# Attention row maxima in one chained pass: bias or mask added on VectorE, with the other part's extreme as the initial value

## The chip, the cores and the metric

One core of a Trainium2 chip runs the whole kernel. The metric is device time in microseconds (us) of one execution. The engines are named as the profile names them: PE (TensorE: matmuls, with PEld for its weight loads), DVE (VectorE), ACT (ScalarE), POOL (GpSimd) and SP (SyncE, which issues most of the transfers).

## The reference, cut to what matters

The model is a two-layer backbone over 512 latent tokens (an 8 x 64 grid) and 256 context tokens, of width 1024 with 16 heads of 64. Each layer is half a SwiGLU, a token mixer and another half SwiGLU. Mixer 0 (layer 0) is a neighbourhood attention with a learned bias; mixer 1 (layer 1) is a windowed attention with grouped keys, a band mask and a sink logit for each head. In both, a latent query also sees all 256 context keys, and one softmax goes over all of it.

```python
# mixer 0, for the query rows r (window of 8 x 32 keys, bias or -1e30 outside)
s_win = einsum('bcqhd,bicjhd->bhcqij', q_r, k_r) + bias
s_ctx = einsum('bcqhd,bkhd->bhcqk', q_r, kc)
p = softmax(concatenate([s_win, s_ctx], -1))
o = p_win @ v_r + p_ctx @ vc
# mixer 1, for each block b of 128 queries (keys of blocks b-1, b, b+1)
s_win = where(abs(pos_q - pos_k) <= 128, einsum('bqhgd,bkhd->bhgqk', qb, kb), -1e30)
s_ctx = einsum('bqhgd,bkhd->bhgqk', qb, kc)
p = softmax(concatenate([s_win, s_ctx, sink], -1))     # the sink takes weight, it has no value
o = p_win @ vb + p_ctx @ vc
```

## The kernel before

Activations are kept with the model's width on the partitions; every fp32 product is made of three matmuls (high by high, high by low, low by high). `ffn` runs the half SwiGLUs "0a", "0b", "1a" and "1b", `na_mixer` mixer 0 and `wa_mixer` mixer 1, in the order 0a, mixer 0, 0b, 1a, mixer 1, 1b. The code issues work in program order, and a scheduler in the framework then sets the order of the instructions on each engine by its own estimate of their times. So attention is mixed on each engine with the projections (`pq`, `pk`, `vn`, `wq`) and with the output projections (`pon`, `pow`) of neighbouring steps. Once set, the order of each engine is fixed: an engine that waits holds up all that stands behind.

The scores are computed negated (the queries are scaled by -0.125), so a row maximum is a minimum here: `m` is min over the row, and ACT computes exp(m - s) with `scale=-1.0`.

Mixer 0, `lat` (L988): for each quarter of the heads (`qd`), pair (`pr`), block of 16 columns (`cb`) and head `h`, one bank of PSUM `s` takes 256 window scores and 256 context scores. DVE then takes the minimum of the context half (L1014), adds the bias to the window half and takes the minimum with it in one pass (L1015, an accumulating pass which the profile shows as two instructions, the pass and a read of the accumulator), and takes the smaller of the two 128x1 values (L1017). ACT does the exponential (L1019), DVE the reciprocal of the sum (L1020), POOL scales (L912), PE transposes (`tp`, L893), DVE or ACT copies the transposed block back (L845, L843), and PE multiplies by the values (`o`, L903).

Mixer 1, `attn` (L1155): for each of eight pairs of heads (`s`), each block `b` of 128 queries and each of its two heads there are `nw` window scores (256 in blocks 0 and 3, 384 in blocks 1 and 2) and 256 context scores. Where they fit one bank, both are in `sw` (blocks 0 and 3); otherwise the context scores are in a bank of their own, `sc` (`split`). The band mask is added on PE: a bf16 identity `idb` times the bf16 mask `mkb` is accumulated onto the first and the last 128 columns of the window (L1178, L1180). DVE takes the minimum of the row (L1188), for split blocks that of the context part too (L1184), and combines it with the sink (L1190 or L1192). ACT does the exponentials (L1200, L1202, L1204), DVE adds up the sums and takes the reciprocal (L1210 or L1213, L1214), POOL scales, PE transposes (`tpw`, `tpc`) and multiplies (`wo`). PSUM has two banks for `s` and two for `c`.

`vtile` hands out 128x256 tiles of the pool "v", nine of them, which hold the values and, in `mod_out`, a temporary.

Of the kernel before, what the change touches and what calls it, by code (L numbers as in the profile page):

```python
# [8 lines left out]
F32 = mybir.dt.float32  # L9
F32R = mybir.dt.float32r  # L10
BF16 = mybir.dt.bfloat16
# [7 lines left out]
P = 128  # L19
# [19 lines left out]
def hybrid_kernel(ctx: ExitStack, tc: tile.TileContext, h0, cc, crow, wmod, wmodt, bmod, lnp, wst,  # L39
# [13 lines left out]
    def t2(nm, tag="t2"):  # L53
        return tp.tile([P, 512], F32, tag=tag, name=nm, bufs={"t2": 6, "ln": 2, "sl": 2}[tag])
# [244 lines left out]
    def mod_out(nm, d, c0, c1, st, prm, rm=False, dd=None):  # L299
# [6 lines left out]
        if nm == "in":  # L306
            uf = t2(f"uf{nm}_{d}", "ln" if d < 3 else "t2")
        elif nm == "l0_1":
            uf = gp.tile([P, 256], F32, tag="gs", name=f"uf{nm}_{d}", bufs=6)
        elif n <= 256:  # L310
            uf = ph["S"].tile([P, 256], F32, tag="v", name=f"uf{nm}_{d}", bufs=9)
        else:
            uf = t2(f"uf{nm}_{d}")
# [29 lines left out]

    last_rstd, last_add, hold, keep_back = [None], [None], [None], [None]
# [540 lines left out]
    def vtile(nm):  # L885
        return ph["S"].tile([P, 256], F32, tag="v", name=nm, bufs=9)
# [55 lines left out]
    def na_mixer(gt):  # L942
# [45 lines left out]
        def lat(qd, pr, st, oh, ol, cbs=range(4)):  # L988
# [15 lines left out]
            for cb in cbs:  # L1004
                pts = []
                qc = slice(cb * P, (cb + 1) * P)
                for h in range(2):
# [8 lines left out]
                                                   scale=1.0, scalar=BIG, op0=ALU.add, op1=ALU.min, accum_out=m[:, 1:2])  # L1016
                    nc.vector.tensor_tensor(out=m[:, 0:1], in0=m[:, 0:1], in1=m[:, 1:2], op=ALU.min)  # L1017
                    p = t2(f"p{nm}")
                    last_exp[0] = nc.scalar.activation(p[:], ps[:], AF.Exp, bias=m[:, 0:1], scale=-1.0, accum_out=l[:, 0:1])  # L1019
# [78 lines left out]

    mkb = cp.tile([P, 2, P], BF16, name="mkb")
    idb = cp.tile([P, P], BF16, name="idb")  # L1100
    nc.vector.tensor_copy(idb[:], idn[:])

    def wa_mixer(gt):
# [6 lines left out]
        mk = t2("mk")  # L1110
        nc.sync.dma_start(mk[:, 0:256], wmask[:])
        nc.vector.tensor_copy(mkb[:].rearrange("p a b -> p (a b)"), mk[:, 0:256])
# [42 lines left out]
        def attn(s, q, oh, ol, bs=range(4), tags=("t", "mm")):  # L1155
# [8 lines left out]
            for b in bs:  # L1164
# [6 lines left out]
                mc, lc = (small("mc", f"mc{nm}"), small("lc", f"lc{nm}")) if split else (None, None)  # L1171
                pw, pc = [], []
                for h in range(2):
                    pb = bank("s", f"sw{nm}_{h}")
                    nc.tensor.matmul(pb[:, 0:nw], q[h][:, qc], k[h][:, k0:k1], start=True, stop=False)
                    nc.tensor.matmul(pb[:, 0:nw], q[h][:, qc], k[2 + h][:, k0:k1], start=False, stop=False)
                    if b > 0:
                        nc.tensor.matmul(pb[:, 0:P], idb[:], mkb[:, 0, :], start=False, stop=b == 3)  # L1178
                    if b < 3:
                        nc.tensor.matmul(pb[:, nw - P:nw], idb[:], mkb[:, 1, :], start=False, stop=True)  # L1180
                    pb2 = bank("c", f"sc{nm}_{h}")[:, 0:NC] if split else pb[:, nw:nw + NC]
                    scores(pb2, q[h], k[h], k[2 + h], qc, slice(NL, NT))
                    if split:
                        nc.vector.tensor_reduce(out=mc[:, h:h + 1], in_=pb2, axis=AX.X, op=ALU.min)  # L1184
                        pc.append(pb2)
                        pb = pb[:, 0:nw]
                    mh = m[:, h:h + 1]
                    nc.vector.tensor_reduce(out=mh, in_=pb, axis=AX.X, op=ALU.min)  # L1188
                    if split:
                        x = nc.vector.scalar_tensor_tensor(out=mh, in0=mh, scalar=mc[:, h:h + 1], in1=sink(h), op0=ALU.min, op1=ALU.min)  # L1190
                    else:
                        x = nc.vector.tensor_tensor(out=mh, in0=mh, in1=sink(h), op=ALU.min)  # L1192
                    pw.append(pb)
# [321 lines left out]
```

## Time and profile before

| | us |
|---|---|
| median of 3 runs | 2760.47 (2759.29 to 2761.58) |
| the profiled execution, its own time | 2773.53 |
| its span in the profile | 2771.7 |
| stretch of mixer 0 (taken as 615 to 1010 us) | 395 |
| stretch of mixer 1 (taken as 2080 to 2360 us) | 280 |
| PE busy over the span | 2659.9 |
| DVE / POOL / ACT busy over the span | 1857.4 / 1674.3 / 1204.9 |

The views used are: the page (busy time of each engine over the span), the busy time by stretch, the groups of instructions by line (count, busy time, mean duration, and the idle time before them with what ended it), the list of who waited for whom, and the timeline, in which each row has start, duration, engine, line, operation, and in brackets the idle time of the engine before it and what ended it. Starts follow each other more closely than durations suggest, since instructions of an engine overlap in its pipeline.

### The profile page before, as it was taken

To read this page: it belongs to the slowest core of one execution; us is meant where nothing else is said; L and a number is where in the kernel's file an instruction comes from. 1 tells how busy PE (TensorE), PEld (TensorE's weight loads), DVE (VectorE), ACT (ScalarE), POOL (GpSimd) and SP (SyncE) were. 2 spreads that over 40 slices of the span, in tenths; PEclk is the share of its full clock that TensorE was granted. 3 is DMA by queue.
4 is the path that set the end of the run, shared out by engine and by line. 5 is a ranking of instruction groups with operands and counts; after the bars stand their busy time and mean duration, and the time that the engine had idled before them with its cause. 6 is when DMAs were issued, how large, how long until landed. Compare 5 with 4: busy or idle time off the path is not lost. (4 is left out here: it accounts for less than half of the span.)

```text
span 2771.7 us, 47917 instructions
## 1 busy us (share of the span) xinstructions
PE 2659.9 (96%) x16954; PEld 2423.5 (87%) x16954; DVE 1857.4 (67%) x4250; ACT 1204.9 (43%) x2493; POOL 1674.3 (60%) x1522
## 2 busy tenths in 40 slices
PE   8999999999999989999999999999998999899997
PEld 5899998888888889999998899999986777898997
DVE  4877777775555677656565776666587667677765
ACT  5334343366446344343433434343336655444442
POOL 4786765464434556867664577767545445667762
PEclk9999999999999999999999999999998999999998
DMA  9367555422222213444453236465722111235551
GB/s 320 105 174 205 143 155 152 144 80 61 58 58 57 63 46 92 117 127 126 125 132 106 73 87 165 112 166 165 205 87 63 32 31 47 63 103 126 133 143 57
DMA packets 295615, 311.92 MB, mean 113 GB/s; under 512 B 27856, under 2 KB 193872, under 8 KB 294352
## 3 DMA queue, kind: packets, MB, share of 16 engines
q1 hardware_dynamic: 278960, 279.36, 33.8%
q0 software_dynamic: 16128, 29.37, 6.3%
q8 instruction: 134, 2.20, 0.3%
q14 instruction: 105, 0.86, 0.1%
q10 hardware_dynamic: 288, 0.14, 0.0%
HBM read 300.92 MB, written 12.25 MB: 113 GB/s over the span
## 5 line engine op out<-in xcount | busy, mean ns | idle before, releaser
L104 POOL TENSOR_TENSOR wl<-wr,wh 128x512 fp32r<-128x512 f32 x200 | 262.7, 1332 | 161.2 <-ACT wh L102 102.7
L104 POOL TENSOR_TENSOR wl_s<-S,wh_s 128x512 fp32r<-128x512 f32 x240 | 316.6, 1354 | 53.5 <-ACT wh_s L102 53.0
L102 ACT CAST wh_s<-S 128x512 fp32r<-128x512 f32 x256 | 155.9, 620 | 430.3 <-POOL S L636 151.2
L636 POOL TENSOR_TENSOR S<-wr,wr 128x512 f32<-128x512 f32 x128 | 173.6, 1356 | 191.8 <-DMA wr<-in_wst_dram 177.5
L211 DVE CUSTOM_DVE_ANT_0 jk<-wt,cb 128x512 f32<-128x512 f32 x360 | 244.5, 679 | 23.7 <-DMA wt<-in_wmodt_dram 18.9
L104 POOL TENSOR_TENSOR wl_a<-wr,wh_a 128x512 fp32r<-128x512 f32 x144 | 189.5, 1364 | 17.9 <-ACT wh_a L102 14.0
L102 ACT CAST wh_a<-wr 128x512 fp32r<-128x512 f32 x192 | 118.9, 622 | 152.8 <-PE pd1b L165 21.8
L102 ACT CAST wh<-wr 128x512 fp32r<-128x512 f32 x200 | 120.3, 617 | 85.5 <-DMA wr<-in_wst_dram 21.9
L495 DVE SCALAR_TENSOR_TENSOR z<-pd0b,gt,z 128x256 f32<-128x256 f32 (+1 forms) x168 | 97.0, 594 | 43.9 <-PE pd0b L166 43.2
L495 DVE SCALAR_TENSOR_TENSOR z<-pd1a,gt,z 128x512 f32<-128x512 f32 (+1 forms) x160 | 95.5, 613 | 39.1 <-PE pd1a L166 38.5
L912 POOL TENSOR_SCALAR p<-p,l 128x512 f32<-128x512 f32 x64 | 44.5, 697 | 110.0 <-DVE l L1020 107.5
L495 DVE SCALAR_TENSOR_TENSOR z<-pd0a,gt,z 128x512 f32<-128x512 f32 (+1 forms) x160 | 93.4, 611 | 16.5 <-PE pd0a L166 16.3
L335 POOL TENSOR_SCALAR z<-z,ag_None,ab_None 128x256 f32<-128x256 f32 (+1 forms) x78 | 62.7, 807 | 63.7 <-DVE uh L321 48.8
L636 POOL TENSOR_TENSOR S<-wr,S 128x512 f32<-128x512 f32 x64 | 90.4, 1413 | 3.5
L636 POOL TENSOR_TENSOR S<-S,wr 128x512 f32<-128x512 f32 x64 | 90.3, 1411 | 2.9
L912 POOL TENSOR_SCALAR pw<-pw,l 128x512 f32<-128x512 f32 (+1 forms) x64 | 41.2, 643 | 66.7 <-DVE l L1214 25.7
L1019 ACT ACTIVATE p<-s,m 128x512 f32<-128x512 f32 x64 | 44.0, 689 | 81.2 <-DVE m L1017 76.5
L317 ACT ACTIVATE ufl<-z,bi_None,sc_None 128x256 f32<-128x256 f32 (+1 forms) x86 | 55.3, 654 | 52.9 <-DVE z L480 51.8
L322 DVE TENSOR_TENSOR ul<-ufl,uh 128x256 fp32r<-128x256 f32 (+1 forms) x88 | 61.0, 699 | 5.1 <-ACT uh L319 3.6
L495 DVE SCALAR_TENSOR_TENSOR z<-pd1b,gt,z 128x512 f32<-128x512 f32 (+1 forms) x91 | 53.2, 618 | 11.2 <-PE pd1b L166 10.4
L211 DVE CUSTOM_DVE_ANT_0 jk<-zspare,cb 128x512 f32<-128x512 f32 x88 | 59.7, 678 | 0.5
L163 PE MATMUL vn<-wh,uh 128*128 128x256 f32 x192 | 54.9, 286 | 1.0 <-DVE nq L856 0.5
(1483 smaller groups left out, 10650.8 us busy)
## 6 DMA issues: line engine op xcount, KB each, us to landing
wr<-in_wst_dram SPq DMA_DIRECT2D x456, 256.0 KB
wt<-in_wmodt_dram SPq DMA_DIRECT2D x206, 256.0 KB
zspare<-in_wmodt_dram SPq DMA_DIRECT2D x50, 256.0 KB
wr_0b<-in_wst_dram SPq DMA_DIRECT2D x47, 256.0 KB
wr_1b<-in_wst_dram SPq DMA_DIRECT2D x47, 256.0 KB
wr_2b<-in_wst_dram SPq DMA_DIRECT2D x47, 256.0 KB
wr_3b<-in_wst_dram SPq DMA_DIRECT2D x47, 256.0 KB
wm<-in_wmod_dram SPq DMA_DIRECT2D x8, 1024.0 KB
```

The costliest lines, as they stand in the source:

```text
L102: nc.scalar.copy(hi[:], src[:])
L104: x = eng.tensor_tensor(out=lo[:], in0=src[:], in1=hi[:].bitcast(F32), op=ALU.subtract)
L163: behind(nc.tensor.matmul(ps, a[0], b[0], start=first, stop=False), in_front[0])
L211: x = nc.vector.tensor_tensor_reduce(out=junk[:], in0=w[:], in1=cb[st], scale=1.0, scalar=0.0, op0=ALU.mult, op1=ALU.add, accum_out=out[st])
L317: nc.scalar.activation(uf[:, :n], zs, AF.Identity, scale=s1, bias=s2)
L322: return hi, nc.vector.tensor_tensor(out=lo, in0=uv, in1=uo.bitcast(F32), op=ALU.subtract)
L335: nc.gpsimd.tensor_scalar(out=zs, in0=zs, scalar1=prm[2][:, d:d + 1], scalar2=prm[3][:, d:d + 1], op0=ALU.mult, op1=ALU.add)
L495: last[0] = nc.vector.scalar_tensor_tensor(out=zt(d, c0, c1), in0=pd, scalar=gt[:, d, st:st + 1], in1=zt(d, c0, c1), op0=ALU.mult, op1=ALU ...
L636: nc.gpsimd.tensor_tensor(out=t[:], in0=a[:], in1=b[:], op=o)
L912: nc.gpsimd.tensor_scalar(out=p, in0=p, scalar1=r, scalar2=0.0, op0=ALU.mult, op1=ALU.add)
L1019: last_exp[0] = nc.scalar.activation(p[:], ps[:], AF.Exp, bias=m[:, 0:1], scale=-1.0, accum_out=l[:, 0:1])
```

## The change

In mixer 0 the accumulating pass (L1015) takes the context minimum `m[:, 0:1]` as its initial value in place of a large constant, so its result `m[:, 1:2]` is the minimum of both halves, and L1017 is gone. In mixer 1 the mask is no longer added on PE. DVE makes two accumulating passes: one over the window scores, which adds the mask `mk3` (fp32: left edge, a block of zeros, right edge) with the sink as its initial value, and one over the context scores, which adds zeros (`nil`) with the first pass's result as its initial value. The plain minima (L1184, L1188) and the small combining steps (L1190, L1192) are gone. Tiles `mkb` and `idb` go, `mk3` takes 1.5 KB in each partition of the mixer's pool, and "v" has eight tiles there. The mask is loaded by two transfers, without a cast, and POOL clears the middle block once.

```diff
@@ lat (mixer 0)
                     nc.vector.tensor_reduce(out=m[:, 0:1], in_=ps[:, 256:512], axis=AX.X, op=ALU.min)
                     nc.vector.tensor_tensor_reduce(out=ps[:, 0:256], in0=ps[:, 0:256], in1=nbs[h][:, (0, 1, 1, 2)[cb], :],
-                                                   scale=1.0, scalar=BIG, op0=ALU.add, op1=ALU.min, accum_out=m[:, 1:2])
-                    nc.vector.tensor_tensor(out=m[:, 0:1], in0=m[:, 0:1], in1=m[:, 1:2], op=ALU.min)
+                                                   scale=1.0, scalar=m[:, 0:1], op0=ALU.add, op1=ALU.min, accum_out=m[:, 1:2])
                     p = t2(f"p{nm}")
-                    last_exp[0] = nc.scalar.activation(p[:], ps[:], AF.Exp, bias=m[:, 0:1], scale=-1.0, accum_out=l[:, 0:1])
+                    last_exp[0] = nc.scalar.activation(p[:], ps[:], AF.Exp, bias=m[:, 1:2], scale=-1.0, accum_out=l[:, 0:1])
@@ wa_mixer
-        mk = t2("mk")
-        nc.sync.dma_start(mk[:, 0:256], wmask[:])
-        nc.vector.tensor_copy(mkb[:].rearrange("p a b -> p (a b)"), mk[:, 0:256])
+        vbufs[0] = 8
+        mk3 = ph["S"].tile([P, 3, P], F32, tag="mk", name="mk", bufs=1)
+        nc.gpsimd.memset(mk3[:, 1, :], 0.0)
+        for i in range(2):
+            nc.sync.dma_start(mk3[:, 2 * i, :], wmask[:, i, :])
+        mk = mk3[:].rearrange("p a b -> p (a b)")
+        nil = mk3[:, 1:2, :].broadcast_to([P, 2, P])
@@ attn (mixer 1)
-                    nc.tensor.matmul(pb[:, 0:nw], q[h][:, qc], k[h][:, k0:k1], start=True, stop=False)
-                    nc.tensor.matmul(pb[:, 0:nw], q[h][:, qc], k[2 + h][:, k0:k1], start=False, stop=False)
-                    if b > 0:
-                        nc.tensor.matmul(pb[:, 0:P], idb[:], mkb[:, 0, :], start=False, stop=b == 3)
-                    if b < 3:
-                        nc.tensor.matmul(pb[:, nw - P:nw], idb[:], mkb[:, 1, :], start=False, stop=True)
+                    scores(pb[:, 0:nw], q[h], k[h], k[2 + h], qc, slice(k0, k1))
                     pb2 = bank("c", f"sc{nm}_{h}")[:, 0:NC] if split else pb[:, nw:nw + NC]
                     scores(pb2, q[h], k[h], k[2 + h], qc, slice(NL, NT))
+                    mh, mk0 = m[:, h:h + 1], 0 if b else P
+                    nc.vector.tensor_tensor_reduce(out=pb[:, 0:nw], in0=pb[:, 0:nw], in1=mk[:, mk0:mk0 + nw], scale=1.0,
+                                                   scalar=sink(h), op0=ALU.add, op1=ALU.min, accum_out=mc[:, h:h + 1])
+                    pb3 = pb2.rearrange("p (a b) -> p a b", a=2)
+                    x = nc.vector.tensor_tensor_reduce(out=pb3, in0=pb3, in1=nil, scale=1.0, scalar=mc[:, h:h + 1],
+                                                       op0=ALU.add, op1=ALU.min, accum_out=mh)
                     if split:
-                        nc.vector.tensor_reduce(out=mc[:, h:h + 1], in_=pb2, axis=AX.X, op=ALU.min)
                         pc.append(pb2)
                         pb = pb[:, 0:nw]
-                    mh = m[:, h:h + 1]
-                    nc.vector.tensor_reduce(out=mh, in_=pb, axis=AX.X, op=ALU.min)
-                    if split:
-                        x = nc.vector.scalar_tensor_tensor(out=mh, in0=mh, scalar=mc[:, h:h + 1], in1=sink(h), op0=ALU.min, op1=ALU.min)
-                    else:
-                        x = nc.vector.tensor_tensor(out=mh, in0=mh, in1=sink(h), op=ALU.min)
```

The scheduler sets the order of the engines anew. The order shows the same instructions elsewhere; it differs in the two mixers and at the seams to the steps around them. Three places follow; line numbers are those of each kernel's own file, and the numbers at the end of a name are buffer numbers.

The first is DVE in mixer 0, first quarter of the heads, first pair, third block of columns (`m0_0_2`), for both heads. Before:

```order
L1014 TENSOR_REDUCE m0_0_2_0_6908<-s0_0_2_0_6903 128x1
L1014 TENSOR_REDUCE m0_0_2_1_6928<-s0_0_2_1_6923 128x1
L1015 ISA s0_0_2_0_6903,m0_0_2_0_6908<-s0_0_2_0_6903,nb0_0_6796 128x256
L1015 ISA m0_0_2_0_6908 128x1
L1015 ISA s0_0_2_1_6923,m0_0_2_1_6928<-s0_0_2_1_6923,nb1_0_6801 128x256
L1015 ISA m0_0_2_1_6928 128x1
L1017 TENSOR_TENSOR m0_0_2_0_6908<-m0_0_2_0_6908 128x1
L1017 TENSOR_TENSOR m0_0_2_1_6928<-m0_0_2_1_6928 128x1
```

And in the changed kernel:

```order
L1014 TENSOR_REDUCE m0_0_2_0_6901<-s0_0_2_0_6896 128x1
L1014 TENSOR_REDUCE m0_0_2_1_6920<-s0_0_2_1_6915 128x1
L1015 ISA s0_0_2_0_6896,m0_0_2_0_6901<-s0_0_2_0_6896,nb0_0_6793,m0_0_2_0_6901 128x256
L1015 ISA m0_0_2_0_6901 128x1
L1015 ISA s0_0_2_1_6915,m0_0_2_1_6920<-s0_0_2_1_6915,nb1_0_6798,m0_0_2_1_6920 128x256
L1015 ISA m0_0_2_1_6920 128x1
```

The first head's value is ready two instructions into the passes, where before it waited behind the second head's pass.

The second is DVE in mixer 1, the fourth pair of heads (`s` = 3), block 1, which is split (`l3_1` are its sums; `pw` and `wol` belong to other steps). Before, from the copy ahead of it to the reciprocal of its first sum:

```order
L845 COPY pw2_3_1_24362<-tpw2_3_1_24377 128x512
L1188 TENSOR_REDUCE m3_1_24445<-sw3_1_0_24450 128x1
L1188 TENSOR_REDUCE m3_1_24445<-sw3_1_1_24461 128x1
L1190 SCALAR_TENSOR_TENSOR m3_1_24445<-m3_1_24445,mc3_1_24448,nsink_82 128x1 x2
L845 COPY pw3_0_1_24416<-tpw3_0_1_24431 128x512
L1210 SCALAR_TENSOR_TENSOR l3_1_24446<-l3_1_24446,lc3_1_24449,le3_1_24447 128x1
L1188 TENSOR_REDUCE m3_2_24515<-sw3_2_0_24520 128x1
L1184 TENSOR_REDUCE mc3_2_24518<-sc3_2_0_24525 128x1
L1214 RECIPROCAL l3_1_24446<-l3_1_24446 128x1
```

And in the changed kernel:

```order
L845 COPY pw2_3_1_24254<-tpw2_3_1_24269 128x512
L1178 ISA sw3_1_0_24341,mc3_1_24339<-sw3_1_0_24341,mk_22790,nsink_82 128x384
L1178 ISA mc3_1_24339 128x1
L1178 ISA sw3_1_1_24349,mc3_1_24339<-sw3_1_1_24349,mk_22790,nsink_82 128x384
L1178 ISA mc3_1_24339 128x1
L1181 ISA sc3_1_0_24344,m3_1_24336<-sc3_1_0_24344,mk_22790,mc3_1_24339 128x256
L1181 ISA m3_1_24336 128x1
L1181 ISA sc3_1_1_24352,m3_1_24336<-sc3_1_1_24352,mk_22790,mc3_1_24339 128x256
L1181 ISA m3_1_24336 128x1
L845 COPY pw3_0_1_24307<-tpw3_0_1_24322 128x512
L909 TENSOR_TENSOR wol1_0_24051<-wo2_0_24054,woh1_0_24050 128x512
```

Before, the context minima `mc3_1` of this block stood much earlier in the order; now the passes over `sc3_1` stand behind those over `sw3_1`.

The third is PE at the same place: the window scores of both heads. Before:

```order
L893 MATMUL tpw2_3_1_24377<-idn_74,pw2_3_1_24362 128x128 x4
L1175 MATMUL sw3_1_0_24450<-wk0_0_23049,wq1_1_0_24042 128x384
L1176 MATMUL sw3_1_0_24450<-wkl0_0_23051,wq1_1_0_24042 128x384
L1178 LDWEIGHTS idb_120
L1178 MATMUL sw3_1_0_24450<-mkb_119,idb_120 128x128
L1180 LDWEIGHTS idb_120
L1180 MATMUL sw3_1_0_24450<-mkb_119,idb_120 128x128
L1175 MATMUL sw3_1_1_24461<-wk1_0_23050,wq1_1_1_24043 128x384
L1176 MATMUL sw3_1_1_24461<-wkl1_0_23052,wq1_1_1_24043 128x384
L1178 LDWEIGHTS idb_120
L1178 MATMUL sw3_1_1_24461<-mkb_119,idb_120 128x128
```

And in the changed kernel:

```order
L893 MATMUL tpw2_3_1_24269<-idn_74,pw2_3_1_24254 128x128 x4
L869 MATMUL sw3_1_0_24341<-wk0_0_22983,wq1_1_0_23948 128x384
L870 MATMUL sw3_1_0_24341<-wkl0_0_22985,wq1_1_0_23948 128x384
L869 MATMUL sw3_1_1_24349<-wk1_0_22984,wq1_1_1_23949 128x384
L870 MATMUL sw3_1_1_24349<-wkl1_0_22986,wq1_1_1_23949 128x384
L893 MATMUL tpw3_0_0_24313<-idn_74,pw3_0_0_24304 128x128 x4
```

The mask matmuls and their weight loads are gone, 96 of each over the mixer, and the scores follow each other directly.

More of the change, by code (lines that the diff above doesn't have):

```diff
@@ L10 @@
 F32R = mybir.dt.float32r
-BF16 = mybir.dt.bfloat16
 I32 = mybir.dt.int32
@@ L310, in mod_out @@
         elif n <= 256:
-            uf = ph["S"].tile([P, 256], F32, tag="v", name=f"uf{nm}_{d}", bufs=9)
+            uf = ph["S"].tile([P, 256], F32, tag="v", name=f"uf{nm}_{d}", bufs=vbufs[0])
         else:
@@ L342, in behind @@
                 mybir.DependencyClass.NoSync, mybir.DependencyReason.DATA), reason="order")
+    vbufs = [9]
     last_rstd, last_add, hold, keep_back = [None], [None], [None], [None]
@@ L885, in vtile @@
     def vtile(nm):
-        return ph["S"].tile([P, 256], F32, tag="v", name=nm, bufs=9)
+        return ph["S"].tile([P, 256], F32, tag="v", name=nm, bufs=vbufs[0])
     def transpose(nm, p, order, tags):
@@ L1096, in na_mixer @@
         wo3(1)
-    mkb = cp.tile([P, 2, P], BF16, name="mkb")
-    idb = cp.tile([P, P], BF16, name="idb")
-    nc.vector.tensor_copy(idb[:], idn[:])
     def wa_mixer(gt):
@@ L1170, in attn @@
                 split = nw + NC > 512
-                mc, lc = (small("mc", f"mc{nm}"), small("lc", f"lc{nm}")) if split else (None, None)
+                mc, lc = small("mc", f"mc{nm}"), small("lc", f"lc{nm}") if split else None
                 pw, pc = [], []
```

## The prediction

> **What bounds the kernel now.** I read the page first, then the busy time by stretch (stretch, length, then PE, PEld, DVE, ACT and POOL busy with instructions, granted PE clock, DMA share, GB/s), and then what PE waits for in the two mixers (total us, times, longest).
>
> ```profile
> PE 2659.9 (96%) x16954; PEld 2423.5 (87%) x16954; DVE 1857.4 (67%) x4250; ACT 1204.9 (43%) x2493; POOL 1674.3 (60%) x1522
> 615.00:1010.00 395.00, 374.81 (x2866) 333.88 (x2865) 234.28 (x636) 193.92 (x452) 190.73 (x211) 0.98 0.23 63
> 2080.00:2360.00 280.00, 257.84 (x1836) 207.26 (x1837) 197.67 (x502) 162.36 (x435) 138.93 (x165) 0.97 0.16 43
> ```
>
> PE is the bound: 96% of the span, and in the mixers all but 395 - 374.8 = 20 us and 280 - 257.8 = 22 us. So only two things can move the time: less work on PE, and shorter or longer waits of PE. DVE is busy 59% of the first stretch and 71% of the second; what it gains or loses counts only where PE ends up waiting for it. Mixer 0's waits of PE that end in the attention's own chain are these:
>
> ```profile
> PE o L903 <- DVE p L845: 3.8, 4, 2.4
> PE tp L893 <- POOL p L912: 3.2, 4, 2.0
> PE s L869 <- ACT p L1019: 2.3, 3, 1.2
> PE s_c L869 <- ACT p L1019: 0.9, 1, 0.9
> ```
>
> That is 10.2 us in 12 waits. And from 2110 us on, in mixer 1:
>
> ```profile
> PE tpw L893 <- POOL pw L912: 3.4, 6, 0.7
> PE sw L1175 <- ACT pw L1200: 3.1, 4, 1.5
> PE wo L903 <- DVE pc L845: 1.4, 1, 1.4
> PE wo L903 <- DVE pw L845: 1.2, 3, 0.9
> ```
>
> Here 9.1 us in 14 waits. All stand behind the row minimum, since exponential, scaling and transposes need it.
>
> **Mixer 1, PE's part.** The 96 mask matmuls go, with their weight loads. In busy time a mask looks like 0.22 us, but instructions overlap, so I take the starts. First the end of a split block's scores with two masks, then a block with one:
>
> ```profile
> 2158.20 0.23 PE L1178 MATMUL sw<-mkb,idb 128*128 128x128 bf16 x1
> 2158.26 0.22 PE L1180 MATMUL sw<-mkb,idb 128*128 128x128 bf16 x1
> 2158.29 0.36 PE L869 MATMUL sc<-wk,wq 128*128 128x256 f32 x1
> 2158.49 0.28 PE L870 MATMUL sc<-wkl,wq 128*128 128x256 f32 x1
> ...
> 2150.39 0.28 PE L1176 MATMUL sw<-wkl,wq 128*128 128x256 f32 x1
> 2150.51 0.23 PE L1180 MATMUL sw<-mkb,idb 128*128 128x128 bf16 x1
> 2150.55 0.36 PE L869 MATMUL sw<-wk,wq 128*128 128x256 f32 x1
> 2150.76 0.28 PE L870 MATMUL sw<-wkl,wq 128*128 128x256 f32 x1
> 2150.88 0.82 PE L893 MATMUL tpw<-idn,pw 128*128 128x128 f32 x6
> ```
>
> A score matmul of 256 columns that follows another takes 0.12 us from start to start (2150.76 to 2150.88, and 2150.39 to 2150.51). With two masks ahead it is 0.29 us from the first mask to L870 (2158.20 to 2158.49): 0.09 for the masks, and 0.20 for the product behind them, which they delay. Without them 0.12 remains, so a pair of masks costs 0.17 us. One mask: 2150.51 to 2150.76 is 0.25, less 0.12 is 0.13. Eight pairs of heads, two heads, two split and two unsplit blocks are 32 pairs and 32 single masks: 32 x 0.17 + 32 x 0.13 = 9.6 us. That is the most that PE's work falls; where PE waits for the chain anyway, it is nothing.
>
> **Mixer 1, DVE's part.** The groups by line and shape (busy us, mean ns | idle before):
>
> ```profile
> L1188 DVE TENSOR_REDUCE m<-sw 128x1 f32<-128x512 f32 x32 | 21.5, 681 | 6.2 <-PE sw L870 6.2
> L1188 DVE TENSOR_REDUCE m<-sw 128x1 f32<-128x384 f32 x32 | 17.3, 547 | 1.5 <-PE sw L1180 1.3
> L1184 DVE TENSOR_REDUCE mc<-sc 128x1 f32<-128x256 f32 x32 | 13.2, 413 | 0.3 <-PE sc L870 0.2
> L1192 DVE TENSOR_TENSOR m<-m,nsink 128x1 f32<-128x1 f32 x32 | 11.6, 366 | 0.2
> L1190 DVE SCALAR_TENSOR_TENSOR m<-m,mc,nsink 128x1 f32<-128x1 f32 x32 | 9.8, 317 | 0.1
> L1015 DVE CUSTOM_DVE_ANT_0 s<-s,nb 128x256 f32<-128x256 f32 x64 | 27.2, 429 | 3.8 <-POOL nb L999 2.7
> L1017 DVE TENSOR_TENSOR m<-m 128x1 f32<-128x1 f32 x64 | 19.1, 299 | 1.1
> L1017 DVE TENSOR_TENSOR m<-m x64: 140/159/1455, 623.5 to 972.0; 128x1 f32<-128x1 f32 x64
> ```
>
> Before, the five kinds of mixer 1 take 21.5 + 17.3 + 13.2 + 11.6 + 9.8 = 73.4 us. After there are 128 passes. Mixer 0's L1015 is the same pass on the same kinds of operand: 429 ns for 256 columns, and its accumulator read 0.14 us (a row below). For 384 columns I add the step of the plain minimum from 256 to 384, 547 - 413 = 134, so 563 ns. Split: 32 x (563 + 140 + 429 + 140) = 40.7 us; unsplit: 32 x 2 x (429 + 140) = 36.4; together 77.1 us, only 3.7 more. The change does remove the separate minimum, but not instructions: 160 become 256.
>
> The chain is worse off than the sum. These rows show the block of the second and third places in the order:
>
> ```profile
> 2212.95 1.01 DVE L1188 TENSOR_REDUCE m<-sw 128x1 f32<-128x384 f32 x2
> 2213.88 0.34 DVE L1190 SCALAR_TENSOR_TENSOR m<-m,mc,nsink 128x1 f32<-128x1 f32 x2
> 2214.27 0.59 ACT L1200 ACTIVATE pw<-sw,m 128x384 f32<-128x384 f32 x1
> 2217.93 0.55 PE L893 MATMUL tpw<-idn,pw 128*128 128x128 f32 x3 [0.71 <-POOL pw L912]
> ```
>
> The exponential starts 1.32 us after the first minimum, because the context's minima had been taken earlier. In the new order the same head needs two window passes with reads and one context pass with its read. Passes overlap by some 0.08 us, as the two minima above do (1.01 against 2 x 547), so about 2 x 0.63 + 0.49 = 1.75 us: 0.43 later. An unsplit head goes by the means from 681 + 366 = 1047 to 2 x 569 = 1138 ns, 0.09 later. The ends for one wait are thus 0.09 and 0.43 us; most listed waits are by split blocks or follow both kinds, so I take 0.3, above the middle. 14 waits x 0.3 = 4.2 us given back (ends 1.3 and 6.0). Elsewhere the longer chain is hidden by other PE work: `pow`, `wq`, the previous block's `wo`.
>
> **Mixer 0.** 64 L1017 go, 19.1 us of DVE. The chain of the first place in the order:
>
> ```profile
> 642.24 0.14 DVE L1015 DVE_READ_ACCUMULATOR2_ANT m<- 128x1 f32 x1
> 642.62 0.33 DVE L1017 TENSOR_TENSOR m<-m 128x1 f32<-128x1 f32 x2
> 642.82 0.69 ACT L1019 ACTIVATE p<-s,m 128x512 f32<-128x512 f32 x1 [2.29 <-DVE m L1017]
> 643.65 0.39 PE L869 MATMUL s<-nk,nq 128*128 128x256 f32 x1 [1.18 <-ACT p L1019]
> ```
>
> The first head's read ends at 642.38, and ACT starts at 642.82, after L1017 of that head. Without it ACT can start some 0.35 us earlier, and PE's wait of 1.18 shrinks by as much. Where the heads are not paired it is the 0.16 of the median. I take 0.3, the mean of L1017, for ten of the twelve waits; the two longest (2.4 and 2.0 us) must hang on something larger. Gain 3.0 us (ends: nothing, and all 10.2).
>
> L1017 has a median of 159 ns, a mean of 299 and a longest of 1455: some of these tiny steps are held up by something, while L1015 with one operand in PSUM averages 429 for 256 columns. [...]
>
> **The rest costs nothing.** One clear of 128x128 on POOL, one more mask load on SP's queue (which stands one place earlier), minus two casts on DVE; the first mask was needed long after its cast:
>
> ```profile
> L1112 DVE CAST mkb<-mk x1: 282/282/282, 2087.3 to 2087.3; 128x256 bf16<-128x256 f32 x1
> L1180 PE MATMUL sw<-mkb,idb x48: 219/219/314, 2118.7 to 2340.6; 128*128 128x128 bf16 x48
> ```
>
> Those 31 us hide the second load and the clear; without that cover they would cost PE well under a microsecond. The load waits for the old owner of its memory, as the old one did; behind it on SP stand weight loads which wait for POOL anyway. Eight instead of nine "v" tiles still leave two beside the six that hold values. Moves of `pon` and of the sums at the end of mixer 0 I price at zero, within plus or minus 4.4 us (the two longest waits above, 2.4 + 2.0, which a new order may remove or repeat).
>
> **Sum.** -9.6 + 4.2 - 3.0 = -8.4 us. Against the profiled execution's 2773.5 that is 2765.1; it ran 13.1 us above the median, and the same step from the median, 2760.5, gives 2752.1, 0.3% less. A change within 0.2% (5.5 us) would be no more than a measurement of this kernel can tell from none.
>
> **Rivals.** First, no change: PE's saving falls largely into stretches where the chain ends last. If half of the masks stand there, PE gains 4.8, gives back 4.2 and mixer 0 brings 1.4: -2.0, or 2758.5. For it: 14 waits spread over the mixer. Against: PE is busy 258 of 280 us. Chance 0.29.
>
> Second, slower: the context scan loses its early place. In each of the 32 split heads the context pass and read (0.49 us) now stand behind the window's. If all are exposed, 32 x 0.49 = 15.7, less 9.6 and 1.4, is 4.7 slower; with more holds of 0.09 in 32 unsplit heads 7.6 slower: 2765 to 2768. It decides above (9.6 + 1.4) / 0.49 = 22 of 32 heads. For it: the order, and one PE wait already at that place. Against: the scheduler has put other matmuls between. Chance 0.14.
>
> Third, the clock. After waits of up to 1.5 us PE's clock fell in this stretch:
>
> ```profile
> 2140.00:2150.00 10.00, 9.21 (x59) 7.51 (x59) 7.51 (x24) 7.49 (x28) 5.49 (x9) 0.66 0.31 79
> ```
>
> A clock of 0.66 over 10 us loses 3.4 us. If longer waits bring two more such stretches, -8.4 becomes -1.6; with the second rival it adds to the loss. Chance 0.05 alone. [...]
>
> **Numbers.** My forecast has 0.52, with its own range 2747 to 2755. Faster by over 0.2% 0.52, within 0.2% 0.32 (first and part of the third), slower 0.16 (second, part of the third). The full bounds are -9.6 - 10.2, or 2741, and 7.6 + 3.4, or 2771; leaving out a tenth on each side, 2743 to 2766.
>
> **What would show it.** In the profile after: no L1178 or L1180 matmuls on PE, and PE instructions down by 96; the new passes near 429 and 563 ns, with no long tail, and DVE's total down by some 15 us (19.1 less 3.7); PE's waits for `p` in mixer 0 below 10 us, and in mixer 1 for `pw` above 9; mixer 1 shorter by some 5 us and mixer 0 by 3. I am wrong if the passes are held up like L1192 was, if PE's waits in mixer 1 grow by 10 us or more, or if the moved work at the end of mixer 0 makes a wait of its own.

## The result and the profile after

The changed kernel takes 2750.97 us, the median of 18 runs (2744.59 to 2760.98), against 2759.56 us for the kernel before (18 runs, 2754.78 to 2767.35): the ratio is 0.997, with a 95% interval of 0.9961 to 0.9979. The prediction said 2752.1. The total came out as forecast, 8.6 us less against 8.4. The sum behind it did not: by the profiles mixer 0 brought some 11 us instead of 3, and mixer 1, which was to bring 5.4, cost about 4.

The page's line of busy times shows 96 instructions fewer on PE; DVE has 30 more and is less busy. (A second profile of the kernel before has DVE at 1850.4, so the fall is 10.6 against that one and 17.6 against the first, which had a step of 7.1 us outside the mixers that the second doesn't show.) Little of that fall is the change's: by the stretches below, DVE's busy time in the two mixers together fell by 5.4 us against the first profile and 4.4 against the second; the rest lies in stretches whose code is all but the same.

```profile
PE 2644.3 (96%) x16858; PEld 2410.4 (88%) x16858; DVE 1839.8 (67%) x4280; ACT 1204.5 (44%) x2493; POOL 1675.8 (61%) x1523
```

To split the time by stage I take landmarks of PE. Mixer 0 is the stretch from the first `pq` matmul to the first `pa0b` (the next half SwiGLU), mixer 1 that from the first `sw` to the last `pow`. In the busy time by stretch (stretch, length, then PE, PEld, DVE, ACT and POOL busy with their instructions, granted clock, DMA share, GB/s), the kernel before:

```profile
566.30:989.50 423.20, 403.45 (x3024) 358.12 (x3025) 251.29 (x677) 217.24 (x495) 205.99 (x222) 0.99 0.22 62
2118.30:2361.20 242.90, 226.62 (x1710) 182.73 (x1709) 168.48 (x440) 140.74 (x392) 123.61 (x153) 0.99 0.16 44
```

The same view of the kernel after:

```profile
561.60:973.30 411.70, 398.60 (x3012) 354.00 (x3012) 240.14 (x610) 217.42 (x495) 204.26 (x220) 1.00 0.23 64
2096.10:2342.90 246.80, 221.01 (x1613) 177.41 (x1613) 174.22 (x535) 140.50 (x392) 124.37 (x153) 0.99 0.16 44
```

Mixer 0 is 11.5 us shorter, mixer 1 is 3.9 us longer. (The shorter count of matmuls in mixer 0 is a move over the seam: 12 `pon` products stand behind the first `pa0b` now. At 0.12 us from start to start they are 1.4 of the 11.5 us.) In mixer 1 PE is busy for 5.6 us less (226.62 to 221.01), but its time without work grows from 242.90 - 226.62 = 16.3 to 246.80 - 221.01 = 25.8 us, by 9.5. Who waited for whom in these stretches of the kernel after (total us, times, longest): first mixer 0, then the longest wait of mixer 1.

```profile
PE o L903 <- DVE p L845: 3.0, 2, 2.6
PE tp L893 <- POOL p L912: 2.2, 2, 1.9
PE s L869 <- ACT p L1018: 1.2, 2, 0.8
PE pk L162 <- DVE nl L864: 1.1, 2, 0.6
PE s_c L869 <- ACT p L1018: 0.7, 2, 0.3
...
PE sw L869 <- ACT pw L1193: 10.6, 13, 1.6
```

PE's waits for `p` in mixer 0 fall from 10.2 to 3.0 + 2.2 + 1.2 + 0.7 = 7.1 us. In mixer 1 the window scores of the next block now wait 10.6 us, in 13 waits, until ACT has emptied their bank; before, that wait was 3.1 us in 4.

The new passes on DVE, in the groups by line and shape (busy us, mean ns | idle before):

```profile
L1015 DVE CUSTOM_DVE_ANT_0 s<-s,nb,m 128x256 f32<-128x256 f32 x64 | 31.1, 489 | 6.6 <-POOL nb L999 5.3
L1178 DVE CUSTOM_DVE_ANT_0 sw<-sw,mk,nsink 128x384 f32<-128x384 f32 x32 | 19.6, 619 | 1.8 <-PE sw L870 1.4
L1181 DVE CUSTOM_DVE_ANT_1 sc<-sc,mk,mc 128x256 f32<-128x256 f32 x32 | 15.5, 488 | 0.7
```

A pass of 256 columns takes 489 ns, and 429 with a constant as its initial value; that of 384 columns 619, where 563 was reckoned. Some 60 ns more stand in each of the 192 passes.

### The profile page after: what moved, and what is told of

Its sections match the earlier page's. It is cut to its first block, busy times and chain, and to the rows that moved or that the text cites. A ratio compares the mean times of both kernels' runs of the same rounds, so it can differ in the third digit from the quotient of the medians.

```text
span 2751.7 us, 47796 instructions
## 1 busy us (share of the span) xinstructions
PE 2644.3 (96%) x16858; PEld 2410.4 (88%) x16858; DVE 1839.8 (67%) x4280; ACT 1204.5 (44%) x2493; POOL 1675.8 (61%) x1523
## 5 line engine op out<-in xcount | busy, mean ns | idle before, releaser
L103 POOL TENSOR_TENSOR wl_a<-wr,wh_a 128x512 fp32r<-128x512 f32 x144 | 189.8, 1365 | 17.2 <-ACT wh_a L101 13.5
L101 ACT CAST wh<-wr 128x512 fp32r<-128x512 f32 x200 | 120.7, 617 | 96.7 <-DMA wr<-in_wst_dram 19.8
L495 DVE SCALAR_TENSOR_TENSOR z<-pd0a,gt,z 128x512 f32<-128x512 f32 (+1 forms) x160 | 93.5, 613 | 16.6 <-PE pd0a L165 16.6
L495 DVE SCALAR_TENSOR_TENSOR z<-pd1b,gt,z 128x512 f32<-128x512 f32 (+1 forms) x91 | 53.4, 621 | 10.4 <-PE pd1b L165 10.2
```

The costliest lines, as they stand in the source:

```text
L101: nc.scalar.copy(hi[:], src[:])
L103: x = eng.tensor_tensor(out=lo[:], in0=src[:], in1=hi[:].bitcast(F32), op=ALU.subtract)
L495: last[0] = nc.vector.scalar_tensor_tensor(out=zt(d, c0, c1), in0=pd, scalar=gt[:, d, st:st + 1], in1=zt(d, c0, c1), op0=ALU.mult, op1=ALU ...
```

## The experiments

Each kernel is timed against the kernel before on the same chip; a profile shows one execution. Executions of one kernel spread over some 15 us, so stages are compared by the landmarks, and totals by the ratios.

**Mixer 0's part alone.** The pass in `lat` takes `m[:, 0:1]`, the exponential reads `m[:, 1:2]`; mixer 1 stays as it was.

```diff
-    scale=1.0, scalar=BIG, op0=ALU.add, op1=ALU.min, accum_out=m[:, 1:2])
-nc.vector.tensor_tensor(out=m[:, 0:1], in0=m[:, 0:1], in1=m[:, 1:2], op=ALU.min)
+    scale=1.0, scalar=m[:, 0:1], op0=ALU.add, op1=ALU.min, accum_out=m[:, 1:2])
...
-last_exp[0] = nc.scalar.activation(p[:], ps[:], AF.Exp, bias=m[:, 0:1], scale=-1.0, accum_out=l[:, 0:1])
+last_exp[0] = nc.scalar.activation(p[:], ps[:], AF.Exp, bias=m[:, 1:2], scale=-1.0, accum_out=l[:, 0:1])
```

> Mixer 0's part alone: the pass takes the context minimum as its initial value, L1017 is gone; mixer 1 as before. The account on record puts 3.0 us of the gain here: 2756.5 us, ratio 0.999. The rival account, from the two profiles (mixer 0 from its first pq to the next step's first pa0b takes 423.2 us before and 411.7 after): nearly all of the gain is here, ratio 0.995 to 0.997, and mixer 0 in its profile near 412 us.

Measured: 2747.45 us, ratio 0.9949 (0.9931 to 0.9967). All of the gain is here; whether more than all, the intervals of this kernel and the changed one, which just overlap, don't tell.

**Mixer 1's part alone.** Everything in the diff but the lines of `lat`.

> Mixer 1's part alone: mask added on VectorE by the two chained passes, no mask matmuls; mixer 0 as before. The account on record: 9.6 saved on TensorE, 4.2 given back, ratio 0.998 (-5.4 us). The rival account, from the two profiles (first sw to last pow 242.9 us before, 246.8 after): mixer 1 gains nothing or loses 2 to 4 us, ratio 1.000 to 1.0015, with about 10 us of TensorE's waits for pw's exponential.

Measured: 2760.77 us, ratio 1.000 (0.9984 to 1.0015): by itself it brings nothing. In its one profile mixer 1 is 247.9 us long, 5 more than before, and shows the wait of `sw` for `pw` again (11.4 us, 14 times); where the rest of that execution made up for the 5 us is not settled.

**Context first.** The two passes of mixer 1 are swapped: the one over the context takes the sink, the one over the window the context's value. In short, not in the code's own words:

```diff
-x: sw <- sw + mk,  initial sink, result mc;  then sc <- sc + 0, initial mc, result m
+x: sc <- sc + 0,   initial sink, result mc;  then sw <- sw + mk, initial mc, result m
```

> The changed kernel with the two passes of mixer 1 in the other order: context first (with the sink as initial value), then window and mask. If the context scan's lost early place is what mixer 1 pays with, the split blocks win it back: 3 to 5 us below the changed kernel, ratio to before 0.995 to 0.996. If the cost is only the longer passes and their reads, or if TensorE hides the chain, it stays within 0.001 of the changed kernel's 0.997.

Measured: 2737.00 us, ratio 0.9905 (0.9887 to 0.9923), the best of all kernels here: it beats the kernel before and the changed one, by more than the 3 to 5 us that the first branch of the expectation had. Its mixer 1 by stretch, and PE's longest wait in it:

```profile
2087.80:2325.80 238.00, 218.33 (x1614) 177.53 (x1613) 164.10 (x535) 140.17 (x392) 124.62 (x153) 0.99 0.17 45
```

```profile
PE sw L869 <- ACT pw L1193: 5.0, 10, 1.2
```

With the same number of instructions as the changed kernel, mixer 1 takes 8.8 us less (246.80 to 238.00), and the wait for `pw` halves. 6.1 of the 8.8 us are PE's time without work (25.8 to 238.00 - 218.33 = 19.7); the other 2.7 are PE's busy time, and why that falls was not found. The timeline shows why PE waits less. In the changed kernel, the two heads of a split block (start, duration, engine, line):

```profile
2191.56 0.62 DVE L1178 CUSTOM_DVE_ANT_0 sw<-sw,mk,nsink 128x384 f32<-128x384 f32 x1
2192.09 0.62 DVE L1178 CUSTOM_DVE_ANT_0 sw<-sw,mk,nsink 128x384 f32<-128x384 f32 x1
2192.63 0.49 DVE L1181 CUSTOM_DVE_ANT_1 sc<-sc,mk,mc 128x256 f32<-128x256 f32 x1
2193.03 0.49 DVE L1181 CUSTOM_DVE_ANT_1 sc<-sc,mk,mc 128x256 f32<-128x256 f32 x1
2193.40 0.59 ACT L1193 ACTIVATE pw<-sw,m 128x384 f32<-128x384 f32 x1
2194.13 0.44 PE L869 MATMUL sw<-wk,wq 128*128 128x384 f32 x1 [0.70 <-ACT pw L1193]
```

With the context first:

```profile
2181.50 0.62 DVE L1181 CUSTOM_DVE_ANT_0 sw<-sw,mk,mc 128x384 f32<-128x384 f32 x1
2182.04 0.62 DVE L1181 CUSTOM_DVE_ANT_0 sw<-sw,mk,mc 128x384 f32<-128x384 f32 x1
2182.76 0.59 ACT L1193 ACTIVATE pw<-sw,m 128x384 f32<-128x384 f32 x1
```

From the start of the first window pass to the first exponential it is 2193.40 - 2191.56 = 1.84 us in the changed kernel and 2182.76 - 2181.50 = 1.26 with the context first, whose scan has been made earlier, as in the kernel before (1.32 there). Of the 10.5 us between this kernel and mixer 0's part alone, mixer 1 holds 243.1 - 238.0 = 5.1 by the profiles; the other half could not be placed.

**The masks back on PE.** The changed kernel with the 96 mask matmuls as well; the mask is added twice, by PE and by the pass.

> The changed kernel with the 96 mask matmuls put back on TensorE beside VectorE's masked passes, so that the mask is added twice. It prices the matmuls alone. If TensorE's time bounds mixer 1, 9.6 us over the changed kernel: ratio to before 1.0005. If the chain through VectorE ends last in most places, 0 to 4 us over it: ratio 0.997 to 0.9985.

Measured: 2752.64 us, ratio 0.9966 (0.9951 to 0.9982), against 0.997 without them. Mixer 1 by stretch, and the wait:

```profile
2103.20:2347.20 244.00, 226.90 (x1710) 183.41 (x1709) 169.34 (x535) 141.11 (x392) 123.64 (x153) 0.98 0.16 44
```

```profile
PE sw L1181 <- ACT pw L1205: 5.0, 7, 1.4
```

PE is busy for 5.9 us more (221.01 to 226.90), and without work for 8.7 us less (25.8 to 17.1). The masks ran in time in which PE otherwise waits: taking them away was worth nothing that these intervals show in this order. At the 9.6 us of the prediction the kernel with masks would be at 1.0005, outside its interval, which leaves room for some 4 us.

**Masks kept, with the context first.** The last two edits together.

> Context first in mixer 1, as in the fastest kernel so far (0.9905), with the 96 mask matmuls put back on TensorE beside VectorE's masked passes (the mask is added twice). With window first they cost nothing measurable. If that was because the chain ended last there, they must cost now, where TensorE waits less for it: 5 to 10 us, ratio 0.992 to 0.994. If they hide anywhere, 0.9905 again.

Measured: 2747.70 us, ratio 0.9953 (0.9936 to 0.9969), where the context first without masks has 0.9905. Mixer 1 by stretch:

```profile
2099.20:2340.90 241.70, 226.00 (x1708) 182.43 (x1709) 165.90 (x535) 139.64 (x392) 124.06 (x154) 0.99 0.17 45
```

Here the masks do cost. PE is busy for 7.7 us more (218.33 to 226.00) and without work for only 4.0 less (19.7 to 15.7), so mixer 1 is 3.7 us longer (241.7 against 238.0). By the ratios it is 0.0048 or some 13 us, more than either branch of the expectation allowed; the two intervals do not meet, but they come from two chips, and what the profiles don't show of the 13 us stays unplaced.

**Context first, plain.** The context's minimum as a plain reduction and a small step that takes in the sink; then one pass over the window.

> Context first in mixer 1, with a plain minimum of the context and a small step for the sink ahead of the one masked window pass, in place of two chained passes. The chain behind the window scores is the same as with context first. If only that chain counts, 0.9905 again (0.989 to 0.992). If VectorE's own time counts, it is a little faster or slower by what the small step of two operands costs beside a pass's read and pointer, at most 2 us.

Measured: 2742.71 us, ratio 0.9938 (0.9922 to 0.9955); mixer 1 241.4 us:

```profile
2093.40:2334.80 241.40, 220.25 (x1613) 178.93 (x1613) 171.71 (x536) 140.28 (x392) 125.93 (x154) 0.98 0.17 46
```

That is outside what either branch expected: slower than the chained form by 0.0033, where 2 us (0.0007) were the most allowed, though the intervals of the two just overlap. The early place of the context brings about half of the step from 0.997 to 0.9905 also without chaining, and 5.4 of the 8.8 us in mixer 1; whether VectorE's own time is the rest (171.7 us busy in mixer 1 against 164.1) was not tested.

**What mixer 0 paid for: an unread minimum.** Mixer 0 as changed, with the 64 small minima left on DVE, their result read by nobody; mixer 1 as before.

```diff
+nc.vector.tensor_tensor(out=sel[:, 0:1], in0=m[:, 0:1], in1=m[:, 1:2], op=ALU.min)
```

> Mixer 0 as changed (the exponential takes the pass's own result), with a small minimum of the same two values kept on VectorE, 64 times, whose result nobody reads; mixer 1 as before. If mixer 0 gained because the exponential no longer waits for that step, the gain of mixer 0's part alone stays: ratio 0.995 to 0.996, mixer 0 near 412 us. If it gained because VectorE has 64 held-up steps less, most is lost: ratio 0.998 to 1.000, mixer 0 near 420 us.

Measured: 2752.80 us, ratio 0.9970 (0.9955 to 0.9985). The group of the small minima, and mixer 0 by stretch:

```profile
L1017 DVE TENSOR_TENSOR sel<-m 128x1 f32<-128x1 f32 x64 | 21.4, 334 | 1.2
```

```profile
558.60:972.60 414.00, 400.67 (x3024) 355.72 (x3025) 256.75 (x677) 217.82 (x496) 205.03 (x221) 1.00 0.23 63
```

DVE has the 21.4 us back, even dearer than before (19.1), and mixer 0 still is 9.2 us shorter than before. Every one of PE's waits for `p` is the same as in the changed kernel (3.0, 2.2, 1.2 and 0.7). Of its 2.3 us over the changed kernel, 1.4 are the 12 `pon` products, which stand ahead of `pa0b` here (3024 matmuls against 3012). But the half SwiGLU behind, which is rid of them, is longer too, 544.7 us against 543.0. And the ratio lies between the two branches of the expectation: about half of the gain is there, and half is not.

**The same minimum on the path.** The line above, but its result written over `m[:, 1:2]`, which the exponential reads.

```diff
-nc.vector.tensor_tensor(out=sel[:, 0:1], in0=m[:, 0:1], in1=m[:, 1:2], op=ALU.min)
+nc.vector.tensor_tensor(out=m[:, 1:2], in0=m[:, 0:1], in1=m[:, 1:2], op=ALU.min)
```

> Mixer 0 with the chained pass, mixer 1 as before, and after each of the 64 chained passes a minimum of m[0] and m[1] written over m[1], which the exponential reads: the result is the same number, the step stands on the path again. The only difference to the kernel with the unread minimum (2752.8 us, mixer 0 414.0 us long from the first pq to the first pa0b) is where the step's result goes. If the place on the path was what mixer 0 paid for, mixer 0 returns to 420 to 424 us, PE's waits for p to 9 to 10 us, and the time to 2757 to 2763, ratio 0.998 to 1.001. If DVE's busy time (21 us of minima) was what it paid for, it stays like the unread minimum: mixer 0 at 412 to 415, ratio 0.995 to 0.998.

Measured: 2760.04 us, ratio 0.9997 (0.9983 to 1.0011). The whole gain is gone, although the minima take less time here than unread:

```profile
L1017 DVE TENSOR_TENSOR m<-m 128x1 f32<-128x1 f32 x64 | 16.0, 251 | 1.1
```

Mixer 0 by stretch is as long as before:

```profile
559.20:981.60 422.40, 401.97 (x3013) 356.84 (x3013) 251.75 (x675) 216.64 (x494) 204.26 (x220) 0.99 0.22 62
```

From the unread minimum to the one on the path, mixer 0 grows by 8.4 us, 7.1 of them PE's time without work (13.3 to 20.4), although DVE's minima take 5.4 us less; PE's waits for `p` go from 7.1 to 11.2. So what mixer 0 paid for is mainly the place of the step on the path to the exponential, not DVE's time.

**Mixer 0's part alone, again,** beside it on the same chip.

> The same kernel as mixer 0's part alone, beside the one above on one chip. If 2747.5 (0.995) was right for it, it comes out at 0.993 to 0.997 again and mixer 0 at 411.7 us; if the lower of the readings, the 11.4 us by the landmarks alone, is nearer, 0.9955 to 0.997.

Measured: 2746.52 us, ratio 0.9940 (0.9917 to 0.9963). The medians of this kernel and the one with the step on the path differ by 13.5 us. In their profiles mixer 0 differs by 10.7 us (411.7 and 422.4) and the half SwiGLU behind it by 3.2 (542.9 and 546.1). These two stretches together take 968.5 us with the step on the path, 958.7 with the unread minimum and 954.6 here: 9.8 of the 13.9 us go with the step's place (some 3.4 of them by the clock, see below). The other 4.1 go with the minimum being there at all, be it by DVE's time or by the other order at the seam; no run parts those two. Mixer 0 here by stretch:

```profile
559.70:971.40 411.70, 398.54 (x3012) 354.02 (x3013) 240.18 (x611) 217.24 (x495) 204.18 (x220) 1.00 0.22 64
```

PE's time without work is 422.40 - 401.97 = 20.4 us with the step on the path and 411.70 - 398.54 = 13.2 without it: 7.3 us are waits. The other 3.4 are PE's busy time for the same work, and that is the clock, which also differs between executions of one kernel (5.1 and 3.4 us lost in mixer 0 in the two profiles of the kernel before). The two slices of 10 us in which it falls, with the step on the path:

```profile
909.00:919.00 10.00, 7.56 (x59) 7.03 (x58) 8.45 (x21) 2.41 (x6) 4.14 (x4) 0.83 0.51 140
949.00:959.00 10.00, 8.85 (x62) 7.86 (x62) 6.41 (x19) 1.84 (x5) 7.28 (x9) 0.66 0.29 79
```

And without it:

```profile
899.00:909.00 10.00, 7.35 (x65) 7.02 (x63) 7.14 (x14) 3.33 (x7) 5.13 (x4) 0.91 0.34 105
909.00:919.00 10.00, 9.25 (x78) 8.27 (x74) 6.93 (x23) 5.83 (x18) 6.88 (x9) 0.92 0.29 81
```

That is (0.17 + 0.34) x 10 = 5.1 us lost to the clock against (0.09 + 0.08) x 10 = 1.7. The chain in the first quarter, with the step on the path:

```profile
634.91 0.48 DVE L1015 CUSTOM_DVE_ANT_0 s<-s,nb,m 128x256 f32<-128x256 f32 x1
635.31 0.49 DVE L1015 CUSTOM_DVE_ANT_0 s<-s,nb,m 128x256 f32<-128x256 f32 x1
635.71 0.34 DVE L1017 TENSOR_TENSOR m<-m 128x1 f32<-128x1 f32 x2
635.91 0.69 ACT L1019 ACTIVATE p<-s,m 128x512 f32<-128x512 f32 x1 [2.37 <-DVE m L1017]
636.75 0.39 PE L869 MATMUL s<-nk,nq 128*128 128x256 f32 x1 [1.27 <-ACT p L1019]
```

The same place in the changed kernel:

```profile
636.82 0.48 DVE L1015 CUSTOM_DVE_ANT_0 s<-s,nb,m 128x256 f32<-128x256 f32 x1
637.22 0.49 DVE L1015 CUSTOM_DVE_ANT_0 s<-s,nb,m 128x256 f32<-128x256 f32 x1
637.39 0.69 ACT L1018 ACTIVATE p<-s,m 128x512 f32<-128x512 f32 x1 [1.94 <-DVE m L1015]
638.23 0.39 PE L869 MATMUL s<-nk,nq 128*128 128x256 f32 x1 [0.84 <-ACT p L1018]
```

The exponential starts 1.00 us after the first pass there, 0.57 here. The first head's minimum stood behind the second head's pass. PE's wait shrinks by the same 0.43 (1.27 to 0.84).

**A cheaper small minimum.** The kernel before with L1017 in the form with one tensor and one scalar per partition, still on the path.

```diff
-nc.vector.tensor_tensor(out=m[:, 0:1], in0=m[:, 0:1], in1=m[:, 1:2], op=ALU.min)
+nc.vector.tensor_scalar(out=m[:, 0:1], in0=m[:, 0:1], scalar1=m[:, 1:2], scalar2=None, op0=ALU.min)
```

> The kernel before with L1017 as an operation with a scalar operand in place of one with two tensor operands; still one step, on the exponential's path, the scheduler's order only a little different. If the step's holds (mean 299 ns against a median of 159) are what mixer 0 paid, the step falls to about 0.15 us and a good part of the 11 us comes back: ratio 0.996 to 0.998. If it is the step's place behind the second head's pass, nothing comes back: 0.999 to 1.001.

Measured: 2750.32 us, ratio 0.9960 (0.9948 to 0.9973), as much as the whole change, where the second branch had nothing. Its profile is of an execution of 2762 us, far above the median, with mixer 0 at 420.4 us; so a second profile of the same kernel followed.

> A second profile of the kernel with the scalar form of the minimum (the step still on the path). If its gain by the median (2750.3) came from mixer 0, this profile shows mixer 0 at 410 to 414 us, and the first one's 420.4 was an accident; if not, it shows 419 to 422 again, and the gain lies outside mixer 0.

Measured: 2749.55 us in this one run, and mixer 0 again 420.3 us long. First the group of the small minima, then mixer 0 by stretch:

```profile
L1017 DVE TENSOR_SCALAR m<-m 128x1 f32<-128x1 f32 x64 | 13.3, 210 | 1.1
```

```profile
561.90:982.20 420.30, 399.78 (x3013) 354.06 (x3013) 246.66 (x674) 218.16 (x495) 204.89 (x220) 1.00 0.22 62
```

The long tail of the steps is gone (their longest is 216 ns, where L1017 reached 1455), but PE is without work for 20.5 us as ever. Of mixer 0's gain this form gives 2 to 3 us, the 12 moved `pon` products and some clock. The rest lies outside: the stretch from `pa0b` to `pa1a` takes 539.8 and 540.5 us in its two profiles, and 544.8 and 548.2 in those of the kernel before. PE is without work there for 5.1 and 5.7 us, against 9.4 and 9.9 before: its waits of `pon` for `z` (1.2) and of `pa0b` for `uh` (1.6) are gone. Why they went with this form was not tested. So by the ratio the first branch came true, and by mixer 0 the second.

**The kernel before, a second profile.**

> A second profile of the kernel before. If the length of a stage belongs to the kernel, mixer 0 is 422 to 424 us again, and the stretch from pa0b to pa1a, 548 us in the first profile against 541 to 545 in the variants, tells what of that belongs to one execution: near 543 if it does, near 548 if it belongs to the kernel.

Measured: 2756.65 us in this run; mixer 0 is 422.6 us long, mixer 1 243.1, the stretch between `pa0b` and `pa1a` 544.8. Mixer 0's length belongs to the kernel: 422.6 to 423.2 in the three profiles with the old mixer 0 (the one of mixer 1's part alone among them), 411.6 to 411.8 in six with the new one, and 413.7 in the seventh, that of the masks put back. Mixer 1's is less firm: of eight profiles with the old code six have 242.3 to 243.1, one 246.1 and one 240.7. The long one is the scalar form's first, in which PE's clock lost 8.5 us in mixer 1 (summed over slices of 10 us), where it lost 3.4 in the kernel before and in the changed one. The short one is that with the step on the path, where six matmuls more lie ahead of the first `sw`. So a single profile can be off by 2 to 3 of the 3.9 us by which mixer 1 grew. Firmer is the exchange of PE's work for waits: PE's time without work in mixer 1 is 16.0 to 16.6 us in all eight, and 25.8 and 25.6 in the two kernels that have the new code (mixer 1 is 5 us longer in the second). Of the stretch between `pa0b` and `pa1a`, 3.4 us of the first profile's 548.2 belonged to that execution.

## Why the prediction was right in sum and wrong in its terms

**Mixer 1, PE's part (-9.6): wrong.** The matmuls went, but PE's busy time fell by only 5.6 us, and all of it turned into waiting. The prediction read the price of a pair of masks off two places where PE was not waiting, and then multiplied by all 64 places. (There the price was right: without masks the two products of `sc` start 0.12 us apart in the changed kernel, at 2136.47 and 2136.59.) The first rival named the mechanism ("PE's saving falls largely into stretches where the chain ends last"), and the run with the masks put back shows it: 96 matmuls more, no time more that the intervals show. With the context first the same masks cost 3.7 us of mixer 1 (0.0048 of the time by the ratios); what work on PE is worth depended on who ended last.

**Mixer 1, the chain (+4.2): too small.** The delay for one split block was well reckoned: 1.75 us from the first pass to the exponential, and 1.84 measured, against 1.32 before. The number of waits was not. Fourteen waits of before were taken as fixed; a longer chain made new ones, and that of `sw` for `pw` alone grew by 7.5 us, PE's time without work by 9.5, just short of the 10 that the prediction had named as a sign of being wrong. The second rival had the mechanism: the context's scan lost its early place. Its loss for mixer 1 alone was 15.7 - 9.6 = 6.1 us; 3.9 were measured in the profile of the changed kernel, 5 in that of mixer 1's part alone. Swapping the passes gave back 8.8 us of mixer 1.

**Mixer 0 (-3.0): a third or a fourth of what it was.** The saving for one wait was sized at 0.3, near the 0.43 of the timeline. But only ten listed waits were allowed to shrink. In the profiles the time without work falls by 19.8 - 13.1 = 6.7 us (by 7.3 between the two kernels of one chip), not only in waits for `p`, which fell by 3.1, but also where DVE had been late for something else. Who waited for whom in mixer 0 of the kernel before had these two, which the prediction did not count:

```profile
PE pq L163 <- DVE nq L856: 2.8, 2, 1.4
PE pk L163 <- DVE nl L864: 2.6, 4, 0.8
```

After, the first is gone and the second is 1.1. DVE makes `nq` and `nl` between the attention's steps, and with the exponentials and releases earlier they are earlier too. The two kernels with the extra minimum bear that out: unread, it leaves these waits as after (none, and 1.1), and on the path it brings back 2.9 and 2.6. On top come 1.7 to 3.4 us of clock (summed over slices of 10 us, 5.1 and 3.4 us were lost in the two profiles of before, 1.7 after), and 1.4 us by the 12 `pon` products that moved behind the seam, which is no gain of the kernel.

**The holds.** The prediction sized ten waits of mixer 0 by L1017's mean of 299 ns, which has the long steps in it (3.0 us); its rivals have 1.4 us there, ten times L1017's shortest of 0.14. No run shows the 1.4. The long steps don't count in mixer 0: with them gone (a mean of 210 ns instead of 299) but the step on the path, PE's time without work there is not shorter (20.5 and 21.7 us, against 19.8 and 20.6 in the two profiles before); with the step off the path it falls to 13.1. The total is another matter, since that form has the ratio 0.9960; by the profiles its gain lies mostly in the half SwiGLU behind, and what part of it the long steps have is open. The steps' long tail was real: with two tensor inputs the longest took 1455 ns, and the form with one tensor input has none (longest 216 and 218 ns). What held single steps up was not shown. Long steps also came up elsewhere: the sums `l<-l,le` behind the new passes rose from a mean of 221 to 402 ns, while with the context first they are at 223.

```profile
L1206 DVE TENSOR_TENSOR l<-l,le 128x1 f32<-128x1 f32 x32 | 12.9, 402 | 11.5 <-ACT le L1197 7.5 <-ACT pw L1193 3.7
```

**The passes' price: too low by 60 ns,** 192 times, because the row it was taken from had a constant where the new passes read a value for each partition (in mixer 0 nothing else of the pass changed, and it went from 429 to 489 ns). DVE's own total hid it: it was to fall by 15 and fell by 10.6 to 17.6, but in the two mixers only by 4.4 to 5.4.

**The clock** did not enter as the third rival had it. In mixer 1, where the waits did grow, it lost 3.4 us before and 3.4 after. In mixer 0, where they shrank, it lost 0 to 5.2 us in six profiles with the step on the path and 1.7 or 1.8 in seven of eight without (5.1 in that of the masks put back): less as a rule, with so wide a spread that it can't be put down to the change.

By the landmarks the terms are -11.5 and +3.9, or -7.6, and 8.6 was measured; the 8.4 forecast were -3.0 and -5.4. Two errors of about 9 us cancelled. That the time was met was luck, and says nothing for the sum.

## What to carry to other kernels

Price an instruction removed from the bounding engine at the places where that engine is not waiting, and ask at each of them which wait comes next; a saving in a stretch that a chain ends is a longer wait (in mixer 1, 5.6 us less work on PE went with 9.5 us more without). A small step counts first by its place on the path of the repeated chain, for every repetition, and only then by its busy time (the same minimum, on the path instead of unread, made mixer 0 8.4 us longer, though DVE spent 5.4 us less on it); the waits listed before do not bound it. When passes are chained, scan first the operand that is ready first: the same instructions in the other order were worth 0.65% of the time here (0.997 and 0.9905), some 18 us, of which the profiles place 8.8 in the mixer.

## What was not expected of the hardware

The accumulating pass over 256 columns took 429 ns with a constant as its initial value (mixer 0 before), and 486 to 489 ns with a value per partition (both mixers after).

PE's clock fell after some waits of about 2 us and not after others. With the step on the path, PE waited 2.03 us, worked for 1.3 us, and waited 0.74 us:

```profile
947.57 1.32 PE L893 MATMUL tp<-idn,p 128*128 128x128 f32 x8 [2.03 <-POOL p L912]
949.64 0.58 PE L869 MATMUL s<-nk,nq 128*128 128x256 f32 x1 [0.74 <-ACT p L1019]
```

The five microseconds from 950 on had a clock of 0.50. In mixer 0's part alone the wait at the corresponding place was 1.90 us, with one of 0.38 behind it, and the clock stayed at 1.00:

```profile
939.39 0.66 PE L893 MATMUL tp<-idn,p 128*128 128x128 f32 x4 [1.90 <-POOL p L912]
941.57 0.66 PE L903 MATMUL o<-p,vtn 128*64 128x128 f32 x8 [0.38 <-DVE p L845]
```

But the length of these waits doesn't decide it. The kernel before has the same two waits, 2.03 and 0.74 us, at this place in both of its profiles; the clock lost 3.4 us there in the first and 1.7 in the second. The scalar form lost 1.7 in its second profile, where the 2.03 stands alone, and nothing in its first, where 0.32 follows 2.02. And with the masks put back a wait of 1.90 was followed by a loss of 1.7, where four other profiles with 1.90 lost nothing. So the same code loses more in one execution than in another, in steps of some 1.7 us, and no run here shows what decides it. The single waits of 2.44 and 2.65 us, which end at 914 and 907 us (the two kernels in the same order), were followed by a loss of 1.7 us in both.
